# A fused decoder block: one down product moved a place later, the turn of u spread out, weights loaded in halves, one weight sum begun later

## The chip, the cores and the metric

The kernel runs on one core of one Trainium2 chip. The metric is the device time of one execution in microseconds (us), lower is better. The engines are TensorE (PE in the profile), VectorE (DVE), ScalarE (ACT), GpSimd (POOL) and SyncE (SP). Each works through its own queue in order, and waits at an instruction whose inputs or buffers aren't ready.

## The reference, cut to what matters

One layer with 256 tokens, model width 2048 and hidden width 8192, all in float32. The mixer is a gated causal convolution; what follows is the MLP, and only the MLP is touched by the change.

```python
def reference(x, c, norm1_g, norm2_g, mod_w, mod_b, mlp_w1, mlp_w2, ...):
    cond = jax.nn.silu(c)
    mod = cond @ mod_w[i] + mod_b[i]
    sh1, sc1, g1, sh2, sc2, g2 = jnp.split(mod, 6, axis=-1)
    h = _rms_norm(x, norm1_g[i]) * (1.0 + sc1) + sh1
    y = _conv_mixer(h, ...)
    x = x + (1.0 + g1) * y
    h = _rms_norm(x, norm2_g[i]) * (1.0 + sc2) + sh2
    u = jnp.square(jax.nn.relu(h @ mlp_w1[i]))
    x = x + (1.0 + g2) * (u @ mlp_w2[i])
```

## The kernel before, in words

**Arithmetic.** Every float32 matrix is split in two parts, `hi` (ACT, a copy to a rounded type) and `lo = w - hi` (DVE), and each product is made of three matmuls, hi·hi, hi·lo and lo·hi (`three`, lines 253 to 257).

**The MLP in 8 chunks.** A chunk is 1024 of the 8192 hidden columns. From chunk 1 on, the up product h @ w1 of a chunk is done with seven block products in place of eight, called P, R, C, A, Q, B and U (lines 334 to 343). R, Q and U need sums of weight blocks: DVE adds them (`add_weights`). P needs one too: its weights come by a load into an "E tile" (`load_e`, SP queue) and a second, accumulating load on top of it (POOL queue). There are two E tiles, for s = 0 and s = 1, and the same tile serves P, R and U of its s in turn. The down product u @ w2 of a chunk is done in four jobs of 512 output columns, written D(chunk, n) here.

**Events and ticks.** The work of PE is a list of events, written out by hand (lines 348 to 358). A *slot* event is half of the weights of one block product at one s: 6 matmuls of 512 columns. A *down* event is a quarter of a D job: 12 matmuls. `SLOTS` gives the order of the 28 slots of a chunk; `LEAD` says after how many slots each D job comes. In the chunks before the last: 7 slots of chunk c+1, D(c,0), 7 slots, D(c,1), 7 slots, D(c,2), 7 slots, D(c,3), and then on with chunk c+2. I call the four runs of 7 slots S0 to S3; S0 is P, P, R, R, C, C, A of s = 0. The number of an event is a *tick*: at tick j the loop (lines 584 to 594) first calls `prepare(j + 5)`, which puts the `hi` and `lo` of the event five places ahead into the queues of ACT and DVE (there are 6 buffers of each), then the tasks that were put down for tick j, then the event's matmuls. So ACT and DVE see one fixed order, and everything put down for a tick stands in line with the `hi` and `lo` of events to come.

**The turn of u.** A chunk's u comes out with tokens on the partitions, and the down product wants hidden columns there. `turn` (lines 496 to 502) does this in five steps at given ticks: store the block-transposed tile to DRAM (ACT's queue, 256 KB), load it back in pieces of 512 bytes (ACT's queue, 256 KB), relu and square (ACT), `u_high` (ACT), `u_low` (DVE). There are four such turns in a chunk, after the last events of A, Q, B and U, all in S3 (`after_slot`, lines 511 to 529). D(c+1,0) needs all four; it stands behind D(c,3) and S0. The D jobs add into PSUM; between two of them ACT copies the sums out to SBUF and the next job's in (`after_down`, `preload`).

**Loads.** Weights come as tiles of 1 MB into five `raw` buffers, in the order in which they are used, all through SP's queue; each load there waits until a buffer comes free, that is until the last `lo` that read it is done, and what stands behind it in the queue waits too. The E loads stand in this queue at the place where `load_e` is called: in `prepare` of the last U event of their s (line 447). Two gate columns a chunk (`mod_col`, DVE, line 704) are done at the first event of D(c,1) and D(c,3).

Of the kernel before, what the change touches and what calls it, by code (L numbers as in the profile page):

```python
# [11 lines left out]
ALU = mybir.AluOpType  # L12
PSUM = bass.MemoryType.PSUM

P = 128
# [43 lines left out]
SPLIT_LOADS = [("col", SC1 * KT + KT - 1), ("col", SH1 * KT + KT - 1), ("first", KT - 1)]  # L59
# [2 lines left out]
LATE_GATE = {("up", 0): [0, 0, 1, 1]}  # L62
CHUNKS = 8
AHEAD = 5
SLOTS = [(0, name) for name in "PRCAQ"] + [(1, "P"), (0, "B"), (0, "U")] + [(1, name) for name in "RCAQBU"]
SUMS = {"R": "C", "Q": "A", "U": "B"}
LEAD = [(7, 14, 21, 28)] * (CHUNKS - 2) + [(9, 20, 28, 28)]


@with_exitstack  # L70
def conv_block(ctx: ExitStack, tc: tile.TileContext, x, vec, dwq, c_row, mod_r, mod_c, w_first, w_in, w_out, w1, w2, out):
    nc = tc.nc
# [41 lines left out]
    for i in range(2):  # L114
        p = ps.tile([P, 2, 2 * T], F32, name="mm", bufs=2)
        for n in range(2):
            at = 8 * i + 4 * n
# [4 lines left out]
    state = {"used": 0}  # L122
# [15 lines left out]
    HALF = KT // 2  # L138
# [8 lines left out]
    def source(key):  # L147
        kind = key[0]
        if kind == "mod":
            return mod_r[ROWS.index(key[1]), key[2]]  # L150
        if kind == "col":
            return mod_c[COLS.index(key[1])]
        if kind == "first":
            return w_first[key[1]]
        if kind == "in":
            return w_in[key[1] + key[2] * KT]
        if kind == "out":
            return w_out[2 * key[1] + key[2]]
        if kind == "up":
            return w1[key[1], key[2], key[3]]  # L160
        if kind == "down":
            return w2[key[1], key[2], key[3]]
        if kind == "x":
            return x
        return vec[:, soon:]
# [4 lines left out]
    def top_up():  # L170
        while todo and waiting[home(todo[0])] < room[home(todo[0])]:
            key = todo.pop(0)
            tag = home(key)
            waiting[tag] += 1
            if tag == "raw":
                raw[key] = wts.tile([P, KT, P], F32, name="raw", bufs=RAW)
            elif tag == "first":
                raw[key] = start_pool.tile([P, 2 * HELD, P], F32, name="first", bufs=FIRST)
            elif tag == "x":
                raw[key] = x_pool.tile([P, KT, T], F32, name="x1")  # L180
            else:
                raw[key] = v2
                with tc.issue_after(state["load"].ins):
                    state["load"] = nc.sync.dma_start(dwq_sb, dwq)
            with tc.issue_after(state["load"].ins) if "load" in state else ExitStack():
                if key in SPLIT_LOADS:
                    first_half = nc.sync.dma_start(raw[key][:, 0:HALF], source(key)[:, 0:HALF])
                    with tc.issue_after(first_half.ins):
                        state["load"] = nc.sync.dma_start(raw[key][:, HALF:], source(key)[:, HALF:])
                else:  # L190
                    state["load"] = nc.sync.dma_start(raw[key], source(key))
# [84 lines left out]
    def flip(dst, src):  # L276
        on_dve_next(nc.vector.transpose, dst, src)
# [67 lines left out]
    def down_order(chunk):  # L345
        return (0, 1) if chunk == 0 else (1, 0)

    events = []
    for chunk in range(CHUNKS):
        downs = [[("down", chunk, n, c, a) for c in down_order(chunk) for a in range(2)] for n in range(4)]  # L350
        slots = [("slot", chunk + 1, name, s, a) for s, name in SLOTS for a in range(2)]
        done = 0
        if chunk < CHUNKS - 1:
            for n, upto in enumerate(LEAD[chunk]):
                events += slots[done:upto] + downs[n]
                done = upto
        else:
            events += list(chain(*downs))
    at_event = {}
    gates_left = [("col", G2 * KT + k) for k in range(2, KT)]  # L360
    for chunk in range(CHUNKS - 1):
        for n in (0, 1) if chunk == CHUNKS - 2 else (1, 3):
            at_event["down", chunk, n, down_order(chunk)[0], 0] = [gates_left.pop(0)]
    assert not gates_left

# [39 lines left out]
    e_tiles = []  # L405

    def load_e(chunk, s):
        key = quad_key(chunk, s, "P")
        with tc.issue_after(state["load"].ins):
            state["load"] = nc.sync.dma_start(e_tiles[s], source(key))  # L410
        for a in range(2):
            ks = slice(a * HALF, (a + 1) * HALF)
            nc.gpsimd.dma_start(e_tiles[s][:, ks], source(quad_key(chunk, s, "A"))[:, ks], accum_op=ALU.add)  # L413
# [20 lines left out]
    def prepare(j):  # L434
        if j >= len(events):
            return
        ev = events[j]
        with urgent():
            w = weights_of(ev)
            hi = wts.tile([P, HALF, P], F32R, name="hi", bufs=6)  # L440
            lo = wts.tile([P, HALF, P], F32R, name="lo", bufs=6)
            on_act_next(hi, w, AF.Copy)
            if j + 1 < len(events) and events[j + 1][0] == "slot" and events[j + 1][2] in SUMS:
                add_weights(events[j + 1])
            on_dve_next(nc.vector.tensor_tensor, lo, w, hi.bitcast(F32), op=ALU.subtract)
            parts[ev] = [[x[:, 4 * kk : 4 * kk + 4, :].rearrange("p k n -> p (k n)") for x in (hi, lo)] for kk in range(2)]
            if ev[0] == "slot" and ev[2] == "U" and ev[4] == 1 and ev[1] < CHUNKS - 1:
                load_e(ev[1] + 1, ev[3])

    def fetch(n):  # L450
        pieces = []
# [10 lines left out]
    def mlp():  # L462
# [4 lines left out]
        banks = {"A": whole[:, 0, :], "R": whole[:, 1, :], "P": accs[0], "U": accs[0], "Q": accs[1]}  # L467
        banks["B"], banks["C"] = [ps.tile([P, 512], F32, name=name, bufs=1) for name in ("small", "row")]
        sp, sa, s2, s4, b1, b2, b3 = room_two
# [3 lines left out]
        def at_tick(j, *fns):  # L473
            tasks.setdefault(j, []).extend(fns)
# [18 lines left out]
        def dve(*args, **kw):  # L493
            return lambda: on_dve_next(tt, *args, **kw)

        def turn(j, ticks, dst, t, b, w):
            stored, loaded, relu, high, low = ticks
            at_tick(j + stored, lambda: flats.append(store_blocks(t, b)))
            at_tick(j + loaded, lambda: load_blocks(w, flats.pop(0)))
            at_tick(j + relu, lambda: square_relu(w))  # L500
            at_tick(j + high, lambda: u_high(dst(), t, w))
            at_tick(j + low, lambda: u_low(dst(), t, w))

        def u_of(chunk, g):
            def tile_of():
                if u2[chunk][g] is None:
                    u2[chunk][g] = new_u(chunk)
                return u2[chunk][g]
            return tile_of

        def after_slot(j, chunk, name):
            if name == "P":
                at_tick(j + 1, lambda: on_act_next(sp, banks["P"], AF.Copy))
            if name == "A":
                at_tick(j + 1, lambda: on_act_next(sa, banks["A"], AF.Copy))
                at_tick(j + 2, dve(s2, sa, banks["R"], op=ALU.subtract), dve(s4, sp, s2, op=ALU.add))
                at_tick(j + 3, dve(s4, banks["C"], s4, op=ALU.subtract), lambda: flip(b1, s4))
                turn(j, (4, 7, 9, 11, 12), u_of(chunk, 1), 0, b1, s4)
            if name == "Q":
                at_tick(j + 1, dve(s2, banks["Q"], s2, op=ALU.add))  # L520
                at_tick(j + 2, lambda: on_dve_next(nc.vector.scalar_tensor_tensor, sp, s2, -1.0, sp, op0=ALU.mult, op1=ALU.subtract),
                        lambda: flip(b2, sp))
                turn(j, (3, 6, 8, 9, 10), u_of(chunk, 1), 1, b2, sp)
            if name == "B":
                at_tick(j + 1, dve(sa, banks["B"], sa, op=ALU.add), lambda: flip(b3, sa))
                turn(j, (3, 5, 8, 9, 10), u_of(chunk, 0), 0, b3, sa)
            if name == "U":
                at_tick(j + 1, dve(s2, banks["U"], s2, op=ALU.add), lambda: flip(b1, s2))
                turn(j, (2, 4, 7, 8, 9), u_of(chunk, 0), 1, b1, s2)

        def slot(j, ev):
            _, chunk, name, s, a = ev
            with tc.issue_after(state["mm_end"].ins):
                for kk, w in enumerate(parts.pop(ev)):
                    three(banks[name], left_of(name, 4 * s + 2 * a + kk), w, s == a == kk == 0, s == a == kk == 1)
            state["mm_end"] = state["three_end"]
            if s == a == 1:
                after_slot(j, chunk, name)

        def down(j, ev):  # L540
            _, chunk, n, c, a = ev
# [38 lines left out]
        residual = {}  # L580
        at_tick(events.index(("down", CHUNKS - 2, 2, 1, 0)) + 1, lambda: preload((CHUNKS - 2, 3)))
        for t, w in enumerate((s4, sp)):
            turn(0, (0, 3, 6, 6, 7), u_of(0, 1), t, (b1, b2)[t], w)
        for j, ev in enumerate(events):
            prepare(j + AHEAD)
            with urgent():
# [204 lines left out]
    for job in jobs:  # L791
        n = quota.get(job, 0)
# [589 lines left out]
```

## Time and profile before

| what | value |
|---|---|
| median of 3 runs | 1188.9 us (1186.01 to 1190.66) |
| the profiled execution's own time | 1189.44 us |
| its span | 1187.7 us |
| PE busy | 1093.0 us, 92% of the span |
| DVE busy | 952.2 us, 80% |
| ACT busy | 678.3 us, 57% |
| mean DMA rate over the span | 277 GB/s |
| the MLP's slots and down jobs | from about 464 us to the end |

A profile shows one execution. Times in its rows are from the span's start. In a timeline row the first number is the start, the second the length, and a bracket gives how long the engine had been idle before and what ended the wait. Matmuls are pipelined and the ends of their rows are modelled: what counts is the distance from one start to the next. 1.7 us of the profiled time lie outside the span.

### The profile page before, as it was taken

The page shows a single profiled execution, that of the slowest core. Times are in us where ns is not written, and L with a number is a line of the kernel's source. Part 1 is how long each engine was busy: PE and PEld are TensorE (multiplying, and loading weights), DVE is VectorE, ACT ScalarE, POOL GpSimd, SP SyncE. Part 2 cuts the span into 40 slices and gives each one's busy share as a digit, 9 for nine tenths or more (in the row PEclk, how much of TensorE's full clock was granted, in tenths as well). Part 3 has the DMA queues.
Part 4 walks back from the last instruction along what each step waited for, and adds up shares of the span by engine and source line. Part 5 has one row for each costly group of instructions (what it writes and reads, how often), then busy time and mean ns, then how long its engine had stood idle before and what let it go on. Part 6 is the DMA issues. An engine that isn't in the chain of part 4 may idle for free.

```text
span 1187.7 us, 15397 instructions
## 1 busy us (share of the span) xinstructions
PE 1093.0 (92%) x5826; PEld 875.5 (74%) x5826; DVE 952.2 (80%) x1194; ACT 678.3 (57%) x950; POOL 227.4 (19%) x148
## 2 busy tenths in 40 slices
PE   7999999998999988899799799799799799988978
PEld 4888866666799966687588588588578578766867
DVE  5677889988767788799699699699789789879754
ACT  4111585645766664654765676567576486476661
POOL 0000366496696341000000000000000000000000
PEclk9999999999999988999899899899999999989989
DMA  9999989897899767588578659668858848956893
GB/s 386 420 420 420 395 338 332 317 370 274 334 354 386 250 217 231 181 292 277 193 254 290 196 207 303 215 227 272 280 179 294 271 159 287 307 187 205 266 187 103
DMA packets 87308, 328.90 MB, mean 277 GB/s; under 512 B 25153, under 2 KB 43073, under 8 KB 52289
## 3 DMA queue, kind: packets, MB, share of 16 engines
q1 hardware_dynamic: 62896, 297.37, 67.7%
q0 software_dynamic: 4032, 14.68, 6.7%
q10 hardware_dynamic: 20306, 15.87, 4.5%
q8 instruction: 45, 0.74, 0.2%
q14 instruction: 29, 0.24, 0.1%
HBM read 315.83 MB, written 12.07 MB: 276 GB/s over the span
## 4 chain that ended last, share of the span: by engine, by line
PE 53%; DMA 21%; DVE 12%; ACT 9%; issue 4%; POOL 1%; ACTq 0%; SPq 0%; POOLq 0%; DVEq 0%
DMA two<-flat 8%; PE mm L256 8%; PE mm L257 8%; PE mm L255 7%; DMA raw<-mod_c 7%; PE mm L238 5%; DVE lo L271 5%; ACT hi L274 4%; DVE raw L704 3%; DMA flat<-two 3%; PE mm L239 2%; DVE two L271 2%; PE acc L235 2%; PE acc L234 2%; PE acc L236 2%
## 5 line engine op out<-in xcount | busy, mean ns | idle before, releaser
L271 DVE TENSOR_TENSOR lo<-raw,hi 128x1024 fp32r<-128x1024 f32 x240 | 288.7, 1220 | 112.0 <-ACT hi L274 110.2
L274 ACT ACTIVATE hi<-raw 128x1024 fp32r<-128x1024 f32 x240 | 244.2, 1051 | 102.5 <-DVE raw L271 45.6
L213 POOL TENSOR_TENSOR lo<-raw,hi 128x1024 fp32r<-128x1024 f32 x63 | 163.6, 2623 | 200.3 <-DMA raw<-w_in 133.0
L256 PE MATMUL mm<-lo,u 128*128 128x512 f32 x448 | 175.5, 392 | 3.8 <-DVE lo L271 3.7
L257 PE MATMUL mm<-hi,u 128*128 128x512 f32 x448 | 175.2, 391 | 3.9 <-DVE u L271 3.9
L255 PE MATMUL mm<-hi,u 128*128 128x512 f32 x448 | 175.6, 392 | 1.6 <-ACT hi L274 1.6
L274 ACT ACTIVATE hi<-s 128x1024 fp32r<-128x1024 f32 x84 | 87.5, 1057 | 126.5 <-DVE s L271 88.4
L704 DVE SCALAR_TENSOR_TENSOR raw<-raw,cond 128x2048 f32<-128x2048 f32 x53 | 130.8, 2472 | 27.9 <-DMA raw<-mod_c 27.9
L413 POOL DMA_DIRECT2D s<-w x28 | 24.7, 1035 | 567.4 <-DMA s<-w 466.6
L271 DVE TENSOR_TENSOR lo<-s,hi 128x1024 fp32r<-128x1024 f32 x84 | 101.9, 1218 | 8.7 <-ACT hi L274 7.4
L256 PEld LDWEIGHTS mm<-lo,u 128*128 128x128 f32 x448 | 84.5, 189 | 23.3 <-DVE lo L271 5.8
L257 PEld LDWEIGHTS mm<-hi,u 128*128 128x128 f32 x448 | 84.5, 189 | 21.8 <-DVE u L271 4.4
L255 PEld LDWEIGHTS mm<-hi,u 128*128 128x128 f32 x448 | 84.6, 189 | 21.4 <-ACT hi L274 3.6
L210 ACT ACTIVATE hi<-raw 128x1024 fp32r<-128x1024 f32 x80 | 80.9, 1050 | 30.7 <-PE mm L238 10.5
L947 DVE SCALAR_TENSOR_TENSOR acc<-u,v,acc 128x256 f32<-128x256 f32 x224 | 94.5, 484 | 1.9
L238 PE MATMUL mm<-hl,hi 128*128 128x512 f32 x224 | 81.7, 405 | 0.0
L271 DVE TENSOR_TENSOR s<-s,raw 128x1024 f32<-128x1024 f32 x56 | 68.3, 1219 | 0.3
L879 PE MATMUL mm<-two,first 128*128 128x256 f32 x256 | 60.1, 389 | 8.8 <-ACT two L910 8.8
L910 ACT ACTIVATE two<-two,modc,amp 128x256 f32<-128x256 f32 x16 | 9.6, 600 | 95.6 <-DVE modc L662 88.5
L239 PE MATMUL mm<-hl,lo 128*128 128x256 f32 x224 | 63.5, 283 | 0.0
L234 PE MATMUL acc<-hl,hi 128*128 128x256 f32 x224 | 63.4, 283 | 0.0
L235 PE MATMUL acc<-hl,hi 128*128 128x256 f32 x224 | 63.4, 283 | 0.0
(240 smaller groups left out, 2285.8 us busy)
## 6 DMA issues: line engine op xcount, KB each, us to landing
raw<-w SPq DMA_DIRECT2D x114, 1024.0 KB, 5.1
raw<-mod_c SPq DMA_DIRECT2D x62, 1024.0 KB, 12.5
raw<-mod_r SPq DMA_DIRECT2D x32, 1024.0 KB, 7.6
raw<-w_in SPq DMA_DIRECT2D x16, 1024.0 KB, 7.0
raw<-w_out SPq DMA_DIRECT2D x16, 1024.0 KB, 6.5
first<-w_first SPq DMA_DIRECT2D x15, 1024.0 KB, 17.2
s<-w SPq DMA_DIRECT2D x14, 1024.0 KB, 7.9
s<-w POOLq DMA_DIRECT2D x28, 512.0 KB, 9.9
```

The costliest lines, as they stand in the source:

```text
L213: end = by.tensor_tensor(lo, w[:, ks, :], hi.bitcast(F32), op=ALU.subtract)
L234: nc.tensor.matmul(out_p, w, m[:, 0:T], start=begin, stop=False)
L235: nc.tensor.matmul(out_p, w, m[:, T : 2 * T], start=False, stop=False)
L238: nc.tensor.matmul(p[:, c, :], hi[:, k % HALF, :], m, start=(k == 0), stop=(k == KT - 1))
L239: state["mm_end"] = nc.tensor.matmul(p[:, c, T : 2 * T], lo[:, k % HALF, :], m[:, 0:T], start=False, stop=(k == KT - 1), skip_group_check= ...
L255: nc.tensor.matmul(p, x_hi, w_hi, start=begin, stop=False, skip_group_check=not grouped)
L256: nc.tensor.matmul(p, x_hi, w_lo, start=False, stop=False, skip_group_check=not grouped)
L257: state["three_end"] = nc.tensor.matmul(p, x_lo, w_hi, start=False, stop=end, skip_group_check=not grouped)
L271: ordered("dve", lambda: call(*args, **kw))
L274: ordered("act", lambda: nc.scalar.activation(*args, **kw))
L704: nc.vector.scalar_tensor_tensor(w, w, 1.0, cb, op0=ALU.mult, op1=ALU.mult, accum_out=acc)
L947: nc.vector.scalar_tensor_tensor(out, s, w, acc, op0=ALU.mult, op1=ALU.add)
```

## The change

Five things change, all in the MLP.

1. `PLACES` takes the place of `LEAD`: D(c,3) moves from its place ahead of S0 of the next chunk to the place behind it, and all other D jobs follow: S0 of chunk c+1, D(c-1,3), S1, D(c,0), S2, D(c,1), S3, D(c,2). In the first group the runs are 10, 9 and 9 slots, with D(0,0), D(0,1) and D(0,2) behind them. The last group ends as before with D(6,2) and D(6,3) behind all slots. Gates go to D(c,0) and D(c,2).
2. The five steps of each turn get later ticks; `late` gives the last chunk's turn other ones. The turned tile is loaded back into the tile that it was stored from.
3. All `down` weights, all but the first `up` weights and the E tiles are loaded in two halves of 512 KB, one DMA each.
4. `load_e` is called in the tick after the last U event (s = 0) and four ticks after it (s = 1).
5. In `SLOTS`, B of s = 0 goes ahead of P of s = 1.

```diff
-SLOTS = [(0, name) for name in "PRCAQ"] + [(1, "P"), (0, "B"), (0, "U")] + [(1, name) for name in "RCAQBU"]
+SLOTS = [(0, name) for name in "PRCAQB"] + [(1, "P"), (0, "U")] + [(1, name) for name in "RCAQBU"]
-LEAD = [(7, 14, 21, 28)] * (CHUNKS - 2) + [(9, 20, 28, 28)]
+PLACES = [[(10, (0, 0)), (19, (0, 1)), (28, (0, 2))]]
+PLACES += [[(7, (c - 1, 3)), (14, (c, 0)), (21, (c, 1)), (28, (c, 2))] for c in range(1, CHUNKS - 1)]
+PLACES[-1] += [(28, (CHUNKS - 2, 3))]
+PLACES += [[(0, (CHUNKS - 1, n)) for n in range(4)]]
...
-                if key in SPLIT_LOADS:
+                if key in SPLIT_LOADS or key[0] == "down" or key[0] == "up" and key[1:3] not in [(0, n) for n in range(4)]:
...
-        for n in (0, 1) if chunk == CHUNKS - 2 else (1, 3):
+        for n in (0, 1) if chunk == CHUNKS - 2 else (0, 2):
...
-        with tc.issue_after(state["load"].ins):
-            state["load"] = nc.sync.dma_start(e_tiles[s], source(key))
+        for a in range(2):
+            ks = slice(a * HALF, (a + 1) * HALF)
+            with tc.issue_after(state["load"].ins):
+                state["load"] = nc.sync.dma_start(e_tiles[s][:, ks], source(key)[:, ks])
...
-            if ev[0] == "slot" and ev[2] == "U" and ev[4] == 1 and ev[1] < CHUNKS - 1:
-                load_e(ev[1] + 1, ev[3])
...
+            def late(usual, at_end):
+                return [usual if chunk < CHUNKS - 1 else at_end]
+
+            if name == "U" and chunk < CHUNKS - 1:
+                at_tick(j + 4, lambda: load_e(chunk + 1, 1))
...
-                turn(j, (4, 7, 9, 11, 12), u_of(chunk, 1), 0, b1, s4)
+                turn(j, (7, 10, *late(18, 12), *late(20, 12), *late(21, 13)), u_of(chunk, 1), 0, b1, b1)
...
-                turn(j, (3, 6, 8, 9, 10), u_of(chunk, 1), 1, b2, sp)
+                turn(j, (6, 9, *late(16, 11), *late(19, 11), *late(20, 12)), u_of(chunk, 1), 1, b2, b2)
...
-                turn(j, (3, 5, 8, 9, 10), u_of(chunk, 0), 0, b3, sa)
+                turn(j, (5, 8, *late(15, 10), *late(18, 10), *late(19, 11)), u_of(chunk, 0), 0, b3, b3)
...
-                at_tick(j + 1, dve(s2, banks["U"], s2, op=ALU.add), lambda: flip(b1, s2))
-                turn(j, (2, 4, 7, 8, 9), u_of(chunk, 0), 1, b1, s2)
+                at_tick(j + 1, dve(s2, banks["U"], s2, op=ALU.add), lambda: flip(s4, s2))
+                turn(j, (4, 7, *late(14, 9), *late(17, 9), *late(18, 10)), u_of(chunk, 0), 1, s4, s4)
...
+            if (name, s, a) == ("U", 0, 1) and chunk < CHUNKS - 1:
+                at_tick(j + 1, lambda: load_e(chunk + 1, 0))
...
-            turn(0, (0, 3, 6, 6, 7), u_of(0, 1), t, (b1, b2)[t], w)
+            turn(0, (0, 4, 8, 8, 9), u_of(0, 1), t, (b1, b2)[t], w)
```

More of the change, by code (lines that the diff above doesn't have):

```diff
@@ L348, in conv_block @@
     events = []
-    for chunk in range(CHUNKS):
-        downs = [[("down", chunk, n, c, a) for c in down_order(chunk) for a in range(2)] for n in range(4)]
-        slots = [("slot", chunk + 1, name, s, a) for s, name in SLOTS for a in range(2)]
+    for at, places in enumerate(PLACES):
+        slots = [("slot", at + 1, name, s, a) for s, name in SLOTS for a in range(2)]
         done = 0
[L353 to L358, printed above, removed]
+        for upto, (chunk, n) in places:
+            events += slots[done:upto] + [("down", chunk, n, c, a) for c in down_order(chunk) for a in range(2)]
+            done = upto
     at_event = {}
```

## The prediction

> **What bounds the kernel now.** I read the page first, then busy time by stages, the waits of a stage without a boundary, and last the boundary's rows, engine by engine. (All rows are of the profile before.)
>
> ```profile
> DMA two<-flat 8%; PE mm L256 8%; PE mm L257 8%; PE mm L255 7%; DMA raw<-mod_c 7%; PE mm L238 5%; DVE lo L271 5%; ACT hi L274 4%; DVE raw L704 3%; DMA flat<-two 3%; PE mm L239 2%; DVE two L271 2%; PE acc L235 2%; PE acc L234 2%; PE acc L236 2%
> ```
>
> ```profile
> core 0: us, PE busy (x) PEld busy (x) DVE busy (x) ACT busy (x) POOL busy (x), PEclk, DMA share, GB/s
> 767.00:862.00 95.00, 86.69 (x362) 68.77 (x361) 79.54 (x78) 60.21 (x76) 3.51 (x4) 0.96 0.74 244
> ```
>
> ```profile
> PE mm L256 <- DVE lo L271: 0.6, 1, 0.6
> ```
>
> The heaviest single line of the chain is the load of the turn, two<-flat. The second fence is one chunk: 360 matmuls (28 x 6 + 16 x 12), and DVE busy 79.5 of 95 us. The third is all that PE waits for in 863.5 to 934 us: 0.6 us. So nearly all loss sits in the rest, S0 and the first down event after it:
>
> ```profile
> 818.67 0.39 PE L256 MATMUL mm<-lo,u 128*128 128x512 f32 x1
> ...
> 819.35 0.39 PE L256 MATMUL mm<-lo,u 128*128 128x512 f32 x1
> ...
> 840.66 0.39 PE L257 MATMUL mm<-hi,u 128*128 128x512 f32 x1
> ...
> 846.49 0.50 PE L256 MATMUL mm<-lo,s 128*128 128x512 f32 x1 [2.08 <-DVE lo L271]
> ...
> 855.63 0.80 PE L255 MATMUL row<-hi,s 128*128 128x512 f32 x1 [4.28 <-ACT hi L274]
> ...
> 862.09 0.40 PE L255 MATMUL mm<-hi,u 128*128 128x512 f32 x1
> ...
> 863.45 0.40 PE L257 MATMUL mm<-hi,u 128*128 128x512 f32 x1
> ```
>
> Undisturbed, three matmuls take 0.68 us, 0.227 each: 1.36 us for a slot event, 2.72 for a down event, 10.9 for a D job, 81.6 for a chunk. From 840.66 to 863.45 lie 45 spacings, 10.2 us of work in 22.8: **12.6 us lost**. 2.1 is a wait for DVE's `lo`, 4.3 one for ACT's `hi`; behind that the 13 spacings to 862.09 take 6.5 instead of 2.95 us, 3.5 lost to half speed; the rest are small waits and restarts.
>
> ```profile
> 846.38 1.28 ACT L274 ACTIVATE two<-two 128x512 f32<-128x512 f32 x2
> ...
> 847.57 1.04 ACT L274 ACTIVATE hi<-raw 128x1024 fp32r<-128x1024 f32 x1
> 853.34 1.29 ACT L274 ACTIVATE two<-two 128x512 f32<-128x512 f32 x2 [4.72 <-DMA two<-flat]
> ```
>
> ```profile
> 568.86 1.29 ACT L274 ACTIVATE two<-two 128x512 f32<-128x512 f32 x2 [4.49 <-DMA two<-flat]
> ```
>
> ```profile
> 1040.74 1.29 ACT L274 ACTIVATE two<-two 128x512 f32<-128x512 f32 x2 [4.04 <-DMA two<-flat]
> ```
>
> ACT explains the 4.3: the relu of the second turn waits 4.7 us for its load, and the `hi` of the events to come stand behind it. The last two rows are the first and last of six such boundaries.
>
> **The turn: moved out of S0.** With D(c,3) behind S0, u is wanted after D, S0, D, S1 (40.8 us) instead of D, S0 (20.4). The load of A's turn now goes out at tick 10 after A, its relu at 18: behind them lie one down event and seven slots, 12.2 us; Q's has 9.5, B's 10.9, U's 12.2.
>
> ```profile
> q1 hardware_dynamic: 2592, 18.88, 55.2%
> q0 software_dynamic: 576, 2.10, 11.7%
> q10 hardware_dynamic: 2688, 2.10, 6.8%
> ```
>
> ```profile
> DMA to landing us min/median/max: 13.2/13.2/13.2
> ```
>
> ```profile
> DMA to landing us min/median/max: 2.8/2.8/2.8
> ```
>
> Over the 95 us, a weight packet (q1, 18 loads, 144 each) takes 0.552 x 95 x 16 / 2592 = 0.324 us of one DMA engine, a turn packet (q10) 0.038. A turn's load has 512 pieces, 32 to an engine. Alone that is 1.2 us, and 2.8 were measured for the load issued at 854.0: 1.6 fixed, if it met no other. If each packet waits for one weight packet, 32 x 0.362 + 1.6 = 13.2; measured 13.2 (issued at 840.1). Half loads halve the mean weight packet to 3.6 KB: scaled between the two rows' 7.3 KB and 0.78 KB, 0.16 us each, an estimate, and the turn's load takes 32 x 0.20 + 1.6 = 8.0. So even Q's 9.5 us cover it. Where they don't, the wait falls in D(c-1,3), where four prepared down events (10.9 us) lie ahead of PE. I take nothing for it, at most 4.
>
> **What stays in S0: DVE's arrears.**
>
> ```profile
> 477.09 5.77 DVE L271 TENSOR_TENSOR lo<-raw,hi 128x1024 fp32r<-128x1024 f32 x5 [0.48 <-ACT hi L274]
> ```
>
> ```profile
> 841.71 2.25 DVE L704 SCALAR_TENSOR_TENSOR raw<-raw,cond 128x2048 f32<-128x2048 f32 x1
> ```
>
> ```profile
> 845.22 2.51 DVE L271 TENSOR_TENSOR lo<-s,hi 128x1024 fp32r<-128x1024 f32 x2
> 848.64 1.23 DVE L271 TENSOR_TENSOR lo<-raw,hi 128x1024 fp32r<-128x1024 f32 x1 [0.91 <-ACT hi L274]
> ```
>
> A `lo` or a sum costs 1.14 us in a stream ((5.77 - 1.22) / 4). S3 and the D behind it carry Q's and U's sums, the eleven small steps of the turns and a gate of 2.3 us, then S0 brings R's sums. The first `lo` of R ends at 846.4, when PE has waited 2.1. None of this moves: a D job still stands between S3 and S0, with a gate at its first event. The 2.1 and 0.5 of small restarts stay, **2.6**. After R everything was late only through ACT, so the rest goes.
>
> ```profile
> 751.51 0.50 PE L256 MATMUL mm<-lo,s 128*128 128x512 f32 x1 [2.09 <-DVE lo L271]
> ...
> 753.16 0.63 PE L256 MATMUL mm<-lo,s 128*128 128x512 f32 x1
> ...
> 756.15 0.43 PE L257 MATMUL row<-hi,s 128*128 128x512 f32 x1
> ```
>
> Half speed can follow a wait this short: here from 753.16 for 7 spacings of 0.43, 1.4 us; behind 846.49 none followed. Halfway, **0.7**. The Trainium skill (TensorE: Matmul & The Clock Gate, "What's actually happening") has the clock drop only after an idle window of about 3.4 us; this row shows a drop after 2.1, and by the page this term would be 0.
>
> **The E tile of s = 1: a new wait.** Before, its load stood early in SP's queue:
>
> ```profile
> 818.10 0.33 SPq L191 DMA_DIRECT2D raw<-mod_c  x1
> ...
> 830.49 0.42 SPq L410 DMA_DIRECT2D s<-w  x1
> ```
>
> ```profile
> DMA to landing us min/median/max: 7.1/8.9/10.6
> ```
>
> ```profile
> DMA to landing us min/median/max: 4.8/4.8/4.8
> ```
>
> (Issues; landing of its two accumulating loads; landing of a lone raw load.) Now, counting loads and freed buffers in the order of the code, it stands behind a load that waits for the first weight of D(c-1,3), behind S0: six `lo` after R's first, 846.4 + 6.9 = 853.3 in this chunk's times. Ahead of it go 1 MB (2.9 us of 16 engines, from q1), then the half (1.45), with 1.9 fixed (4.8 - 2.9): lands at 859.6; accumulated 7.1 later, 866.7; the second half, issued 0.6 and landing 3.5 longer after issue, by 870.8. PE wants P1 after five slots, a D and five slots from 846.4: at 870.9, its second event at 872.3. With `hi` and `lo` (1.04 + 1.22) on top, the first is ready at 869.0, in time, the second at 873.1, 0.8 late. DVE, which after nine more `lo` and sums (10.3) would be there at 863.6, idles some 4 us of the 5.5 a chunk leaves it (81.6 + 3.4 - 79.5), and may pay for that in later arrears, 1.2: **2.0** (0 if the loads land early; the longest landings are priced as a rival). Moving B ahead of P gives this sum two events; without it the term were 4.7. E of s = 0 goes out behind the load that Q's last `lo` releases, 818.1 in these times (first row); its second half lands by 818.1 + 2.9 + 2.9 + 1.9 = 825.8, is summed by 836.4 and split by 838.7, where before that `lo` ended at 840.4:
>
> ```profile
> 839.22 1.22 DVE L271 TENSOR_TENSOR lo<-s,hi 128x1024 fp32r<-128x1024 f32 x1
> ```
>
> So nothing for it.
>
> So a boundary keeps 2.6 + 0.7 + 2.0 = 5.3 of 12.6: 7.3 less, six times, **44**.
>
> **Half loads on the queues.** SP issues 16 more DMAs a chunk at 0.42: with the 18 of now 14 us in 82. DMA time: 16 x 288 packets of 0.164 instead of 16 x 144 of 0.324: 9 more, 0.6 on 16 engines, on a share of 0.74 x 95 = 70 of 82. Nothing.
>
> **The places that occur once.**
>
> ```profile
> 489.92 0.77 PE L257 MATMUL mm<-hi,u 128*128 128x512 f32 x1 [3.92 <-DVE u L271]
> ```
>
> ```profile
> 1076.75 0.54 PE L255 MATMUL acc<-hi,hl 128*128 128x512 f32 x1 [4.07 <-ACT two L274]
> ```
>
> ```profile
> L274 ACT ACTIVATE two<-acc 128x512 f32<-128x512 f32 x7 | 4.0, 576 | 0.0
> ```
>
> ```profile
> 1134.27 1.29 ACT L274 ACTIVATE two<-two 128x512 f32<-128x512 f32 x2 [3.91 <-DMA two<-flat]
> ```
>
> ```profile
> 1136.74 0.79 PE L255 MATMUL mm<-hi,s 128*128 128x512 f32 x1 [6.40 <-ACT mm L274]
> ```
>
> The first D(0,0) waits 3.9 for u: three more slots stand ahead (4.1 us) and two more `lo` ahead of u_low (2.3), so 2.1 stay; with some half speed, **3** won. U waits 4.1 for the copy of P in the last group, whose run is 11 slots; with D after seven it goes, with half speed after it **5.5** won. But in the first group U now follows P directly: its copy (0.58) stands behind a `hi` (1.04) whose buffer P's last event frees, so 1.9 at least, 5.8 if as above: **3** lost. The last turn: PE waits 6.4 for a preload behind a relu that waits for its load. There everything moves one to three ticks later, and U's load gets two down events (5.4 us) until its relu: with landings of 2.8 to 13.2 between 3 won and 8 lost: **0**.
>
> Sum: 44 + 3 + 5.5 - 3 = 49.5; the profiled execution's 1189.4 - 49.5 = 1139.9, and the median lay 0.5 lower: **1139**.
>
> **The rivals.** *Cleaner* (0.15): E is never late, half speed rarely follows, the last 2.6 shrink to 1.0 as relu and u_low leave S0. For: DVE works only 79.5 of 82. 6 x 11.6 + 5.5 = 75, 1114. *Turn still seen* (0.06): ACT's waits return in D(c-1,3) and half of 12.6 stays: 38 + 5.5, 1146 at best, 1158 with E's 2. *E late* (0.15), the one that ends slower: P is the wait in place of the turn. If a half load takes as long as E's whole load did and each accumulating one as long as the longest shown in this chunk,
>
> ```profile
> DMA to landing us min/median/max: 8.2/8.2/8.2
> ```
>
> ```profile
> DMA to landing us min/median/max: 9.5/11.8/14.1
> ```
>
> then P1's second event is ready at 853.3 + 8.2 + 1.4 + 14.1 + 2.3 = 879.3, 7.0 late, and P's of s = 0 at 818.1 + 8.2 + 1.4 + 14.1 + 2.3 = 844.1, 3.7 late, which DVE in arrears hands on to PE. With half speed (3.5) and 2.6 that is 16.8 a boundary, 4.2 more than now: 1189.4 + 25 - 5.5 = 1209. It decides from about 6 us of lateness at both together. Against: these landings fell beside 1 MB loads. In its milder half it ends between 1160 and 1183. *Packets no cheaper* (0.04): a 4 KB packet costs what q0's packet of 3.6 KB costs, 0.117 x 95 x 16 / 576 = 0.309. Then DMA needs 70 + 16 x 144 x 0.294 / 16 = 112 us a chunk: 17 more than now, 1189 + 100 = 1290. Against: q10's price per byte, and q0 also reads what it adds to. The Trainium skill (DMA: Bandwidth & Descriptors, "Rules for kernel authors") asks for at least 1 MiB per DMA for full bandwidth, which speaks for this rival; no run here shows halves yet.
>
> **The numbers.** Forecast 0.60, its own range 1120 to 1168 (E's term 0 to 6, the last turn). Range for all: 1108 to 1177. Under 0.5% (6 us) a measurement of this kernel can't tell a change. Faster: 0.60 + 0.15 + 0.06 + 0.06 of E late = 0.87; same 0.03; slower 0.06 + 0.04 = 0.10.
>
> **What would show it.** Right: chunks of about 87 us, no ACT wait on two<-flat that PE feels, PE's 2 us before R's `lo` still there, waits of 1 to 2 us at P of s = 1. Wrong: a wait of over 4 us at P, weight loads landing in over 9 us in a row, or a DMA share near 1.

## The result and the profile after

The changed kernel takes **1206.0 us** (median of 4 runs, 1202.5 to 1210.3), the kernel before 1188.8 in the same session (4 runs, 1186.0 to 1190.7): ratio **1.0148**, 95% interval 1.0109 to 1.0188. It is slower by 17 us; the forecast was 1139, 50 us faster, and the time lies outside the range.

The profiled execution of the kernel after took 1210.3, its span 1208.5. Its lines are shifted: L271 (DVE) is now L274, L274 (ACT) L277, the three matmuls L255 to L257 are L258 to L260, the E load L410 is L411, the accumulating load L414, the half loads L190 and L192. The chain that ended last now has another first line:

```profile
DMA s<-w 10%; DVE lo L274 10%; ACT hi L277 6%; DVE s L274 4%; DMA raw<-w 3%; DMA two<-flat 2%; DMA flat<-rowsb 2%; DVE raw L710 2%; DVE two L274 2%; PE mm L260 1%; PE mm L259 1%; PE mm L258 1%; DVE raw L274 1%; ACT x L277 1%; DMA flat<-two 1%
```

The load of the turn (two<-flat), 8% before, has 2%: its wait has left the boundaries. In its place stands s<-w, the E tile. Engine by engine (us in total, times, longest), what ACT and PE waited for in the kernel after:

```profile
ACT hi L277 <- DMA s<-w: 63.5, 17, 7.0
ACT two L277 <- DMA two<-flat: 16.7, 3, 6.5
ACT mm L277 <- DMA flat<-rowsb: 5.0, 5, 1.1
```

```profile
PE acc L258 <- ACT hi L277: 27.3, 8, 4.8
```

The three waits for two<-flat that are left all lie at the end of the kernel. PE's new wait is an `acc` one, which is P. Here it is in the chunk that the prediction worked through, PE's waits first:

```profile
846.04 0.51 PE L259 MATMUL mm<-lo,s 128*128 128x512 f32 x1 [2.08 <-DVE lo L274]
854.25 0.50 PE L259 MATMUL mm<-lo,u 128*128 128x512 f32 x1 [0.77 <-DVE lo L274]
876.41 0.79 PE L258 MATMUL acc<-hi,hl 128*128 128x512 f32 x1 [4.41 <-ACT hi L277]
...
878.26 0.63 PE L260 MATMUL acc<-hi,hl 128*128 128x512 f32 x1
878.69 0.63 PE L258 MATMUL acc<-hi,hl 128*128 128x512 f32 x1
```

R still waits 2.1 for DVE, as forecast. The first event of D(c-1,3), the second row, waits only 0.8. Then P of s = 1 waits 4.4, and the matmuls behind it come every 0.43 us: half speed. The six such waits are 3.9, 4.8, 4.0, 4.4, 1.2 and 3.8.

A measure for the whole kernel is used from here on: the time from the first matmul of R (s = 0) in group 2 to the one in group 7, divided by five, called **the chunk time**. Its ends before and after are

```profile
560.58 0.39 PE L255 MATMUL mm<-hi,s 128*128 128x512 f32 x1
...
1032.10 0.39 PE L255 MATMUL mm<-hi,s 128*128 128x512 f32 x1
```

```profile
556.68 0.39 PE L258 MATMUL mm<-hi,s 128*128 128x512 f32 x1
...
1033.97 0.39 PE L258 MATMUL mm<-hi,s 128*128 128x512 f32 x1
```

so 94.3 before and 95.5 after, where the prediction had about 87. A chunk's undisturbed work is 81.6: 12.7 lost before (the prediction read 12.6), 13.9 after.

The second measure is **loss**: for each pair of matmuls in a row, what their starts lie apart beyond 0.227 us, summed over the matmuls of an event, from the first matmul of the first group to the end. In all it grew from 103.5 to 122.9. Its parts that moved:

| | before | after |
|---|---|---|
| groups 2 to 7 (the boundaries, with small losses between them), without U in the last | 76.7 | 82.4 |
| of it P of s = 1, six | 0 | 42.5 |
| D(0,0) waits for u | 6.1 | 2.1, and 2 in front of it |
| U in the last group | 5.9 | 0 |
| U behind P in the first group | 0 | 8.0 |
| D(7,0), the last turn | 9.1 | 23.2 |

Two rows show the last two lines, the longest wait of each in the kernel after:

```profile
511.00 0.79 PE L258 MATMUL acc<-hi,hl 128*128 128x512 f32 x1 [6.05 <-ACT two L277]
...
1148.03 0.80 PE L258 MATMUL mm<-hi,s 128*128 128x512 f32 x1 [4.77 <-ACT s L277]
```

### The profile page after: what moved, and what is told of

Its sections match the earlier page's. It is cut to its first block, busy times and chain, and to the rows that moved or that the text cites. A ratio compares the mean times of both kernels' runs of the same rounds, so it can differ in the third digit from the quotient of the medians.

```text
span 1208.5 us, 15630 instructions
## 1 busy us (share of the span) xinstructions
PE 1097.5 (91%) x5826; PEld 877.7 (73%) x5826; DVE 951.7 (79%) x1194; ACT 677.9 (56%) x950; POOL 227.0 (19%) x148
## 4 chain that ended last, share of the span: by engine, by line
DVE 19%; DMA 18%; ACT 8%; issue 6%; PE 6%; SPq 1%; ACTq 1%; DVEq 0%; POOLq 0%
DMA s<-w 10%; DVE lo L274 10%; ACT hi L277 6%; DVE s L274 4%; DMA raw<-w 3%; DMA two<-flat 2%; DMA flat<-rowsb 2%; DVE raw L710 2%; DVE two L274 2%; PE mm L260 1%; PE mm L259 1%; PE mm L258 1%; DVE raw L274 1%; ACT x L277 1%; DMA flat<-two 1%
## 5 line engine op out<-in xcount | busy, mean ns | idle before, releaser
L274 DVE TENSOR_TENSOR lo<-raw,hi 128x1024 fp32r<-128x1024 f32 x240 | 287.0, 1219 | 97.2 <-ACT hi L277 93.6
L277 ACT ACTIVATE hi<-raw 128x1024 fp32r<-128x1024 f32 x240 | 240.2, 1048 | 69.4 <-DVE raw L274 36.0
L277 ACT ACTIVATE hi<-s 128x1024 fp32r<-128x1024 f32 x84 | 89.0, 1061 | 194.3 <-DVE s L274 111.1
L260 PE MATMUL mm<-hi,u 128*128 128x512 f32 x448 | 175.3, 391 | 1.8 <-DVE u L274 1.8
L258 PE MATMUL mm<-hi,u 128*128 128x512 f32 x448 | 176.2, 393 | 0.3 <-ACT hi L277 0.3
L274 DVE TENSOR_TENSOR lo<-s,hi 128x1024 fp32r<-128x1024 f32 x84 | 102.4, 1219 | 44.7 <-ACT hi L277 43.2
L414 POOL DMA_DIRECT2D s<-w x28 | 24.4, 873 | 595.2 <-DMA s<-w 571.6
L258 PEld LDWEIGHTS mm<-hi,u 128*128 128x128 f32 x448 | 85.0, 190 | 19.6 <-ACT hi L277 1.6
L260 PEld LDWEIGHTS mm<-hi,u 128*128 128x128 f32 x448 | 84.7, 189 | 19.0 <-DVE u L274 2.2
L213 ACT ACTIVATE hi<-raw 128x1024 fp32r<-128x1024 f32 x80 | 81.0, 1050 | 31.1 <-PE mm L241 10.5
L258 PE MATMUL acc<-hi,hl 128*128 128x512 f32 x112 | 50.7, 453 | 39.0 <-ACT hi L277 27.3
L241 PE MATMUL mm<-hl,hi 128*128 128x512 f32 x224 | 81.6, 405 | 0.0
L274 DVE TENSOR_TENSOR s<-s,raw 128x1024 f32<-128x1024 f32 x56 | 68.3, 1220 | 0.3
L238 PE MATMUL acc<-hl,hi 128*128 128x256 f32 x224 | 63.5, 284 | 0.0
L239 PE MATMUL acc<-hl,lo 128*128 128x256 f32 x224 | 63.5, 284 | 0.0
```

The source lines that it names most:

```text
L213: state["w_hi"] = nc.scalar.activation(hi, w[:, ks, :], AF.Copy).ins
L238: nc.tensor.matmul(out_p, w, m[:, T : 2 * T], start=False, stop=False)
L239: state["mm_end"] = nc.tensor.matmul(out_p, lo[:, k % HALF, :], m[:, 0:T], start=False, stop=end)
L241: nc.tensor.matmul(p[:, c, :], hi[:, k % HALF, :], m, start=(k == 0), stop=(k == KT - 1))
L258: nc.tensor.matmul(p, x_hi, w_hi, start=begin, stop=False, skip_group_check=not grouped)
L260: state["three_end"] = nc.tensor.matmul(p, x_lo, w_hi, start=False, stop=end, skip_group_check=not grouped)
```

## The experiments

The theory after the result: the moved D(c,3) does what it was said to, and four things eat it: the E tile of s = 1 comes late (42 us of loss), the last turn's ticks, U behind P, and perhaps the half loads. The first rival: the moved D brings nothing, as another wait stands right behind the one removed. The second: the halves do the harm. Each kernel below ran with the kernel before on the same chip; the ratio is to that, with its interval. Two kernels whose intervals overlap, some 4 us apart, aren't told apart by their times.

| kernel | us | ratio | chunk time |
|---|---|---|---|
| after | 1206.0 | 1.0148 [1.0109, 1.0188] | 95.5 |
| E early | 1190.5 | 1.0006 [0.9988, 1.0023] | 92.4 |
| end as before | 1197.5 | 1.0065 [1.0041, 1.0089] | 94.8 |
| whole loads | 1197.9 | 1.0071 [1.0046, 1.0097] | 93.9 |
| first group 14 | 1201.8 | 1.0102 [1.0071, 1.0133] | 95.1 |
| gates early | 1197.3 | 1.0076 [1.0050, 1.0102] | 94.7 |
| before, in halves | 1195.8 | 1.0067 [1.0044, 1.0089] | 94.3 |
| core | 1161.4 | 0.9760 [0.9733, 0.9786] | 91.0 |
| core, stores early | **1144.6** | 0.9626 [0.9600, 0.9651] | 88.0 |
| core, stores early, E late | 1192.8 | 1.0033 [1.0018, 1.0048] | 96.1 |
| core, stores early, in halves | 1152.0 | 0.9685 [0.9662, 0.9708] | 87.9 |
| core, stores early, column moved | 1149.1 | 0.9661 [0.9634, 0.9687] | 88.7 |
| core, stores early, column moved, gates early | 1148.9 | 0.9662 [0.9644, 0.9679] | 89.4 |

### The E tile of s = 1 at its old place

```diff
+            if ev[0] == "slot" and ev[2:] == ("U", 1, 1) and ev[1] < CHUNKS - 1:
+                load_e(ev[1] + 1, 1)
...
-            if name == "U" and chunk < CHUNKS - 1:
-                at_tick(j + 4, lambda: load_e(chunk + 1, 1))
```

> The change with one part undone: the E tile of s = 1 is loaded from the place it had before (with the hi and lo of the last U event) and not four ticks after it. Theory (the sum for P of s = 1 comes too late, because its load stands behind a load that waits for the weight of the down product behind S0): the six waits of PE at P of s = 1, which with half speed cost 5.8 to 8.1 us each in the change's profile, 42 in all, go; about 1166. If some of it comes back as arrears of VectorE, 1166 to 1175. Rival (VectorE is the bound, and the wait only moves to another event): under 10 us less, 1196 or more.

1190.5: 15.5 less than the changed kernel, not 40. The loss at P of s = 1 fell from 42.5 to 2.9, as expected; but in D(c,3), nearly all at its first event, it rose from 5.0 to 23.2. PE, then ACT, in a boundary of this kernel show why (ACTq rows are the DMAs that ACT issues):

```profile
845.43 0.50 PE L258 MATMUL mm<-hi,u 128*128 128x512 f32 x1 [2.32 <-ACT hi L277]
```

```profile
835.19 0.33 ACTq L284 DMA_DIRECT2D flat<-rowsb  x1
...
842.75 0.38 ACTq L288 DMA_DIRECT2D rowsb<-flat  x1
843.17 1.23 ACT L277 ACTIVATE mm<-x 128x512 f32<-128x512 f32 x2 [3.14 <-DMA flat<-rowsb]
844.34 1.04 ACT L277 ACTIVATE hi<-raw 128x1024 fp32r<-128x1024 f32 x1
```

B's tile is stored at 835.2 and loaded back at 842.8. The load must wait until the store has landed, ACT issues it, and ACT takes its work in order: 3.1 us, with the `hi` of D(c,3) behind it. In the kernel after, where P holds everything up, the store had mostly landed by then (5.0 in all, 1.1 at most). The Trainium skill (Perfetto Trace Analysis, "Tensor Engine Instruction (MATMUL, LD_WEIGHTS)") calls ACT strict FIFO; the trace agrees, as the `hi` at 844.3 needs nothing of that store and still comes behind it. So half of the first rival is true.

### The last chunk's turn at its old ticks

```diff
-                turn(j, (7, 10, *late(18, 12), *late(20, 12), *late(21, 13)), u_of(chunk, 1), 0, b1, b1)
+                turn(j, (7, 10, 18, 20, 21) if chunk < CHUNKS - 1 else (4, 7, 9, 11, 12), u_of(chunk, 1), 0, b1, b1)
...
```

Q, B and U likewise.

> The change with the ticks of the last chunk's turn as before (store 2 to 4, load 4 to 7, relu 7 to 9 after the last event), all else changed. In the change's profile PE loses 23 us ahead of and in D(7,0), before 9. Theory (the later ticks do it): 14 us less, about 1192. Rival (the small store of the gates, issued in the middle of these loads, makes them land in 11 to 17 us, whatever the ticks): at most 5 less.

1197.5: 8.5 less, where 14 were expected. The end's loss fell from 23.2 to 12.6, with 4.0 of that now in D(6,3).

### Whole loads

```diff
-                if key in SPLIT_LOADS or key[0] == "down" or key[0] == "up" and key[1:3] not in [(0, n) for n in range(4)]:
+                if key in SPLIT_LOADS:
```

and the E tile in one DMA again.

> The change with weights and E tiles loaded whole, 1 MB per DMA. Theory (the late sum): its first half now waits for a whole E load, the turn's loads take 13 us in place of 6, so 0 to 12 us more, 1206 to 1218. Rival (the halves themselves do harm: in the change 512 KB take 6 to 7 us to land where 1 MB took 5): 10 us less or more than that, 1196 or below.

1197.9: 8 less. The theory had expected up to 12 us more, so the second rival has a part: the loss at P of s = 1 is 30.9 instead of 42.5.

### The first group 14, 7, 7

```diff
-PLACES = [[(10, (0, 0)), (19, (0, 1)), (28, (0, 2))]]
+PLACES = [[(14, (0, 0)), (21, (0, 1)), (28, (0, 2))]]
```

> The change with 14, 7 and 7 slots ahead of D(0,0), D(0,1) and D(0,2) in place of 10, 9 and 9, so that D(0,0) stands between P and U, which use one PSUM bank. Theory (PE waits 6.0 us there for the copy of P, and runs at half speed behind it, 8 us in all): 8 us less, about 1198. Rival (VectorE is behind at that place in any case, and the wait moves to the next slot): 2 us less or nothing.

1201.8: 4 less, which the intervals don't tell from nothing. In the profile a down job stands between P and U again, U's loss of 8 went to 0, and D(0,0) still lost only 1.7.

### The gates' store one job earlier

```diff
-                if job == (CHUNKS - 2, 2):
+                if job == (CHUNKS - 2, 1):
```

> The kernel changed with the store and load of the last chunk's gates one job earlier, away from the last turn. Theory (that store shares the queues with the end's turn loads, which land in 11 to 17 there): the end's loss falls from 23 to 12 to 15: 1196 to 1198. Rival (the later ticks alone): within 3 of the kernel changed.

Only the store moves; the load that reads it back stays at its job. 1197.3: 8.7 less, D(7,0)'s loss 15.1 instead of 23.2. The last turn in the kernel after, on ACT:

```profile
1128.87 0.43 ACTq L288 DMA_DIRECT2D two<-flat  x1
1136.52 1.29 ACT L277 ACTIVATE two<-two 128x512 f32<-128x512 f32 x2 [4.68 <-DMA two<-flat]
...
1146.03 1.29 ACT L277 ACTIVATE two<-two 128x512 f32<-128x512 f32 x2 [5.46 <-DMA two<-flat]
...
1158.66 1.29 ACT L277 ACTIVATE two<-two 128x512 f32<-128x512 f32 x2 [6.54 <-DMA two<-flat]
```

The load issued at 1128.87 took

```profile
DMA to landing us min/median/max: 17.1/17.1/17.1
```

and the small gates store went out at 1131.9, amid that. But in the last kernel of the table the same move gained no time, so it isn't shown that this store is what delays the loads.

### Half loads alone, in the kernel before

```diff
-                if key in SPLIT_LOADS:
+                if key in SPLIT_LOADS or key[0] == "down" or key[0] == "up" and key[1:3] not in [(0, n) for n in range(4)]:
```

and the E tile in two halves.

> The kernel before with its weights and E tiles loaded in halves, nothing else. The turn's loads should land in 6 to 8 instead of 13, so the relu's waits of 4 to 5 at six boundaries shrink or go: 6 x 4.3 with some half speed, 20 to 35 less: 1155 to 1170. If halves delay the weights as they seemed to behind the moved D (8 less with whole loads there), that comes off: 1170 to 1185. Rival (the turn isn't helped, the weights are later): 1189 to 1200.

1195.8: 7 more, against the theory. The turn's loads did land faster here: by the DMA issues of 560 to 1060 us (KB, median us to landing), of this kernel,

```profile
two<-flat ACTq DMA_DIRECT2D x22, 256.0 KB, 3.8
...
flat<-rowsb ACTq DMA_DIRECT2D x5, 256.0 KB, 11.7
```

where they were, of the kernel before,

```profile
two<-flat ACTq DMA_DIRECT2D x22, 256.0 KB, 7.1
...
flat<-rowsb ACTq DMA_DIRECT2D x5, 256.0 KB, 4.1
```

But the store of B's tile, in the same boundary, lands in 11.7 instead of 4.1, and ACT waits for both in turn, in the kernel with halves:

```profile
850.25 1.29 ACT L274 ACTIVATE two<-two 128x512 f32<-128x512 f32 x2 [3.30 <-DMA two<-flat]
852.24 0.38 ACTq L285 DMA_DIRECT2D two<-flat  x1
852.66 1.06 ACT L274 ACTIVATE hi<-raw 128x1024 fp32r<-128x1024 f32 x1 [1.12 <-DMA flat<-rowsb]
```

The chunk time stayed 94.3. The 7 us are elsewhere: D(7,0) lost 16.6 instead of 9.1.

### Core: the moved D and its turn, nothing else

The kernel after with whole loads, both E loads and the order of P and B as before, 14, 7, 7 in the first group and the end's old ticks. It is the first four edits above (the gates' store stays where it was) and

```diff
-SLOTS = [(0, name) for name in "PRCAQB"] + [(1, "P"), (0, "U")] + [(1, name) for name in "RCAQBU"]
+SLOTS = [(0, name) for name in "PRCAQ"] + [(1, "P"), (0, "B"), (0, "U")] + [(1, name) for name in "RCAQBU"]
...
+            if ev[0] == "slot" and ev[2] == "U" and ev[4] == 1 and ev[1] < CHUNKS - 1:
+                load_e(ev[1] + 1, ev[3])
```

> The kernel before with only D(c,3) one group later and the middle turns' new places; old order of the slots, whole loads, both E loads at their old place, the end's turns and the first group as before. Theory (the moved D is a gain, and the other parts eat it): the kernel changed less 15.5 (P's waits without the late E load), 8.5 (end), 4 (first group), and 0 to 8 for the halves: 1170 to 1178. Rival (the moved D itself brings nothing, as ACT's wait for B's store at B's load takes the place of the turn's wait): 1185 to 1192.

**1161.4**, 27 less than before. The moved D, with its turn, is a gain by itself; the rival's 1185 is out. D(c,3) still loses 25.0, by ACT's wait for the store:

```profile
1008.51 1.06 ACT L277 ACTIVATE hi<-raw 128x1024 fp32r<-128x1024 f32 x1
1013.00 0.38 ACTq L288 DMA_DIRECT2D rowsb<-flat  x1
1013.42 1.23 ACT L277 ACTIVATE mm<-x 128x512 f32<-128x512 f32 x2 [3.85 <-DMA flat<-rowsb]
```

### Core with the stores early

```diff
-                turn(j, (7, 10, 18, 20, 21) if chunk < CHUNKS - 1 else (4, 7, 9, 11, 12), u_of(chunk, 1), 0, b1, b1)
+                turn(j, (4, 10, 18, 20, 21) if chunk < CHUNKS - 1 else (4, 7, 9, 11, 12), u_of(chunk, 1), 0, b1, b1)
...
```

Q's store goes from 6 to 3, B's from 5 to 3, U's from 4 to 2; loads and relus stay.

> The run before this one, with the four stores of the middle turns two to three ticks earlier, so that none stands right ahead of its load on ACT. If ACT's wait for the store (3.1 us in the chunk looked at) is what holds the `hi` of D(c,3), the waits of 1.5 to 5.5 at D(c,3)'s first event go, 12 to 20 in all: 1155 to 1165. If they come from DVE's arrears at R alone, under 5 less than the run before this one.

**1144.6**, 17 less again and 44 less than before, below the 1155 to 1165 expected, and the best of all kernels. D(c,3) lost 0.4 in all. Its chunk time goes from

```profile
546.62 0.39 PE L258 MATMUL mm<-hi,s 128*128 128x512 f32 x1
...
986.82 0.39 PE L258 MATMUL mm<-hi,s 128*128 128x512 f32 x1
```

88.0: 6.4 lost of the 12.7. The prediction kept 5.3, of which 2.0 for E, and E is early here, so 3.3 is the number to compare. R's wait for DVE, with the half speed behind it, is 3.4 a boundary (20.4 of loss in six). The other 3 us the prediction didn't have: at P of s = 0, in front of R, PE waits 1.1 for DVE in five of the six boundaries (a loss of 6.7 in six), and small waits lie at R of s = 1 and at the first events of D(c,0) and D(c,1). First P's row, then R's, in the profile of this kernel

```profile
807.04 0.47 PE L258 MATMUL acc<-hi,hl 128*128 128x512 f32 x1 [1.08 <-DVE two L274]
...
812.34 0.50 PE L259 MATMUL mm<-lo,s 128*128 128x512 f32 x1 [2.07 <-DVE lo L274]
...
813.84 0.63 PE L259 MATMUL mm<-lo,s 128*128 128x512 f32 x1
...
816.40 0.63 PE L259 MATMUL row<-lo,s 128*128 128x512 f32 x1
```

with half speed that begins 1.5 us behind it.

### The late E tile, alone, in that kernel

```diff
-            if ev[0] == "slot" and ev[2] == "U" and ev[4] == 1 and ev[1] < CHUNKS - 1:
+            if ev[0] == "slot" and ev[2] == "U" and ev[3:] == (0, 1) and ev[1] < CHUNKS - 1:
...
+            if name == "U" and chunk < CHUNKS - 1:
+                at_tick(j + 4, lambda: load_e(chunk + 1, 1))
```

> The run with the stores early, with the E tile of s = 1 loaded after its group's last U event, as in the kernel changed, but whole and with P still ahead of B. By the prediction's own times this is 4.7 a boundary, 28 in all: 1172. Theory (the late load costs what P of s = 1 waited in the kernel changed with whole loads, 5 a boundary, and 2.7 for P's two events earlier): 7 to 8 a boundary, 42 to 47: 1186 to 1192. Rival (P's wait there came from other arrears, and the load is nearly in time here): under 1160.

1192.8: **48 more** by this one edit, 8.0 a boundary, and the whole gain is gone. By the prediction's own 4.7 it would have been 28. P of s = 1 lost 41.0. SP, POOL, ACT and PE of this kernel in one boundary:

```profile
845.67 0.43 SPq L409 DMA_DIRECT2D s<-w  x1
```

```profile
854.51 1.75 POOL L412 DMA_DIRECT2D s<-w  x2 [49.17 <-DVE lo L274]
```

```profile
863.10 1.06 ACT L277 ACTIVATE hi<-s 128x1024 fp32r<-128x1024 f32 x1 [8.76 <-DMA s<-w]
```

```profile
864.21 0.80 PE L258 MATMUL acc<-hi,hl 128*128 128x512 f32 x1 [4.97 <-ACT hi L277]
```

The accumulating load goes out 8.8 after the issue of the plain one, which landed in 8.2 (the row names a `lo` that ended just then), and `hi` begins 8.6 later: 17.4, where PE wanted P 13.6 after the issue (864.2 less the wait of 5.0). So the lateness needs neither halves nor the other order of P and B.

### Halves in that kernel

The edit of the kernel before in halves.

> The run with the stores early, with weights and E tiles in halves. Theory (halves by themselves cost time, as 7 did in the kernel before): 1148 to 1153. Rival (they cost only where ACT waits for a store right ahead of a load): within 2 of 1144.5.

1152.0: 7.5 more. The chunk time is 87.9, no longer at all; so in the middle halves cost nothing. The two profiled executions lie 11.0 apart, and these are places that occur once: D(7,0)'s loss is 15.5 instead of 7.9, and the first group begins 4.2 later, at 467.6, where ACT waits longer for the first E tile (ACT of the kernel in halves, then with whole loads; in the kernel before, the same edit moved this start by only 0.5):

```profile
466.52 1.06 ACT L277 ACTIVATE hi<-s 128x1024 fp32r<-128x1024 f32 x1 [4.63 <-DMA s<-w]
```

```profile
462.33 1.06 ACT L277 ACTIVATE hi<-s 128x1024 fp32r<-128x1024 f32 x1 [0.91 <-DMA s<-w]
```

### The gate column moved, and with it the gates' store

```diff
-        for n in (0, 1) if chunk == CHUNKS - 2 else (0, 2):
+        for n in (0, 1):
```

> The run with the stores early, with the second gate column of a chunk at D(c,1) instead of D(c,2), so that its 2.3 us of DVE no longer stand right ahead of S0. If these make R's first `lo` 2.1 late, the wait goes, with the half speed behind it 2 to 3.5 a boundary: 1125 to 1133. If DVE is behind anyway (77.5 of 82 us a chunk), the wait only moves: 1140 to 1145.

1149.1, 4.5 more, and none of the time that was hoped for; the intervals overlap. R's wait went, but DVE is as late one event earlier, at P, where the read of a bank before P's first matmul stands behind the eleven steps of the turn:

```profile
902.12 0.47 PE L258 MATMUL acc<-hi,hl 128*128 128x512 f32 x1 [2.49 <-DVE two L274]
```

The chunk time is 88.7 instead of 88.0, and D(7,0) lost 11.3 instead of 7.9.

> The run with the gate column moved, and also the store of the last chunk's gates one job earlier. If that store delays the last turn's loads (10 to 15 waited there in other runs, 6 in the run with the stores early), 2 to 5 less than the run with the column moved; if the load is late by its own tick, the same within 2.

With the gates' store one job earlier as well, 1148.9: no difference in time, but one in place. D(7,0)'s loss went from 11.3 to 0, and D(6,3)'s from 1.2 to 11.5. PE, then ACT:

```profile
1085.83 0.79 PE L258 MATMUL mm<-hi,u 128*128 128x512 f32 x1 [8.46 <-ACT mm L277]
```

```profile
1082.56 0.38 ACTq L288 DMA_DIRECT2D two<-flat  x1
```

The store of A's tile went out at 1070.15 and took 12.4, until 1082.55; ACT issued its load then, and had stood idle for 8.0. So at the end, too, ACT waited for a store at its load, at the old ticks of the last chunk. Why that store took 12.4 isn't shown.

## Why the prediction was wrong

**Right.** The turn: moving D(c,3) behind S0 hides the load, and no relu waits for it in the six boundaries. R's 2.1 and half speed stayed, 3.4 a boundary in the core with early stores, for 3.3. U in the last group won 5.9, for 5.5; D(0,0) won 4.0, 2 of which went to the slots in front of it, for 3.

**Too large: the gain of the moved D.** "After R everything was late only through ACT, so the rest goes" did not hold. In the kernel with whole loads, early E and early stores a chunk gained 6.3; without its 2.0 for E the prediction had 9.3. That this kernel is 44 us faster and that the prediction's boundaries came to 44 is chance: its six boundaries bring some 39, of loss, and U in the last group and D(0,0) another 10, which the prediction counted beside its 44.

**Wrong, and it decided: "The E tile of s = 1: a new wait".** Priced at 2.0 a boundary, it cost 7.1 after the change (42.5 / 6), and 8.0 by itself, in whole tiles, with the old order of P and B, for which the prediction had 4.7. (Taken out of the changed kernel alone it gives back only 15.5, as the wait for the store comes up in its place.) Three landings were too short, counted in the chunk above from the end of R's first `lo` (846.4 in the prediction, 846.0 now):

```profile
855.36 0.33 SPq L190 DMA_DIRECT2D raw<-w  x1
855.74 0.43 SPq L192 DMA_DIRECT2D raw<-w  x1
856.21 0.91 SPq L411 DMA_DIRECT2D s<-w  x2
```

```profile
864.41 0.86 POOL L414 DMA_DIRECT2D s<-w  x1 [37.14 <-DMA s<-w]
```

```profile
875.30 1.06 ACT L277 ACTIVATE hi<-s 128x1024 fp32r<-128x1024 f32 x1 [6.78 <-DMA s<-w]
```

The release came 9.3 after R's `lo` instead of 6.9: 2.4 late, as DVE waited 2.2 for ACT's `hi` on the way. From there to the half's landing it took 9.0 instead of 6.3: 2.7. The accumulation, priced at the shortest landing that the prediction had quoted (7.1, of up to 14.1), took 10.9: 3.8. So the first `hi` begins 9.0 late in all, and 9.0 less the 1.9 that the prediction had spare, less 1.5 that PE itself came later, less the `lo` (1.2) that PE's first matmul doesn't need, is the 4.4 that PE waited. Half speed and the second event make 7.1 of it. The prediction had this very case as its rival *E late*, at 0.15, and priced it within 3 us of the result (1209). Its mechanism was half right, since PE waits only for the tile of s = 1, and the number was luck: it had 16.8 lost a boundary, where 13.9 were, and 3 at the end and at U in the first group together, where 22 were. Against it stood that the long landings fell beside 1 MB loads. In halves the same chunk's two E loads, and then the two accumulating ones, landed in

```profile
DMA to landing us min/median/max: 7.6/8.0/8.4
```

```profile
DMA to landing us min/median/max: 10.8/11.4/11.9
```

all the same.

**Wrong: the last turn, 0 with at most 8 lost.** It lost 14.1 more: three loads of the turn there landed in 11.2, 17.1 and 11.3 us, one of them beyond the 13.2 that bounded them. The old ticks give back 8.5 of it.

**Wrong: U behind P in the first group, 3 with at most 5.8.** It lost 8.0, which went to 0 with the old places (4 us of time, within the intervals). The wait for the copy was 6.05, and half speed followed.

**Wrong: "Half loads on the queues. Nothing."** 7 to 8 us, three times. Where the E tile was in time none of it lay in the middle; in the kernel after it lay at P (42.5 of loss there, 30.9 with whole loads). The DMA engines' work is about right: over 88 us of the middle (packets, MB, share of 16 engines) q1 had, in the core with early stores in halves, then with whole loads,

```profile
q1 hardware_dynamic: 4896, 18.88, 60.6%
```

```profile
q1 hardware_dynamic: 2592, 18.88, 57.9%
```

a packet of half the size took 0.174 us for 0.315 (60.6% of 88 x 16, over 4896), 11% over half. So *Packets no cheaper* is out, and the rule of 1 MiB (the Trainium skill, DMA: Bandwidth & Descriptors, "Rules for kernel authors") shows here as 5% more of that queue's time. That the 7 to 8 us come from these 5% isn't shown. The turn's loads landed within the 8.0 of the prediction (medians of 5.9 and 6.8 between 560 and 1060 us of the kernel after), but halves aren't the reason: with whole loads the same medians were 5.4 and 6.3.

**Left out: the store.** The prediction looked at the tick of each load and relu, and not at what the load itself waits for. In the kernel after, ACT's wait for the store is 5.0 in all; with P in time it is 23 to 25 of loss for PE, and a store two or three ticks earlier cures it.

The parts taken back one at a time (15.5, 8.5, 8 and 4) sum to 36, the core gained 44.6. The 8.6 between them have no shown cause: each part is a difference to the same four runs of the changed kernel, which spread over 8 us, and the core also puts back the order of P and B and the load of E of s = 0, which were not tried by themselves. Why the last turn's loads land in 11 to 17 us stays open.

## What to carry to other kernels

When a wait is taken off an engine that works in order, follow that engine's next two waits, the DMAs that it issues and what these wait for included: here the store that the next load waits for was worth 17 us, and the cure was an edit of four numbers. A load that is moved behind the release of a buffer has the whole chain in front of its user (release, load, accumulation, split); price it by the longest landings measured in that stage, and if the slack is less than their spread, leave the load where it was: here that one step was worth 48 us, more than the gain it came with.

## What was not expected of the hardware

- One edit of one queue's packets moved two neighbours in opposite ways, and only in one kernel: with halves in the kernel before, the turn's loads landed in 3.8 instead of 7.1 us and the store of B's tile in 11.7 instead of 4.1; in the core with early stores it was 7.8 for 7.7 and 6.7 for 6.1 (medians between 560 and 1060 us). So packet size alone doesn't give a landing time here.
- Behind a 2.07 us wait PE ran at full speed for 1.5 us and then at half speed for some 3 (813.84 to 816.8, 0.43 a matmul).
- Halved plain loads do little for the 512 KB accumulating loads beside them: between 560 and 1060 us the median was 10.1 before, 9.4 with halves alone and 10.2 after.
